# Second pass over a hand-written order: which column runs before the second U columns, pieces in sequence, later value transposes, first weights split on VectorE

## The chip, the cores and the metric

The kernel runs on one core of a Trainium2 chip. The metric is device time in microseconds (us), the median of several runs. One further execution is taken by the hardware profiler; its own time is given beside the runs. Engines are named as in the profile: PE is TensorE's matmul queue and PEld its weight loads, DVE is VectorE, ACT is ScalarE, POOL is GpSimd, SP is SyncE, which here only issues DMAs.

## The reference

One step of a hybrid decoder layer on a prompt of 1024 tokens and on 8 sampled tokens. What matters here is the first stage: the input is normalised, projected with one weight matrix, and a part of the columns (called u) feeds a recurrence over time, RWKV-7.

```
h = rms_norm(x, ln_g) @ w_in                     # 1024 tokens x 3480 columns
q_raw, kv_raw, g_raw, z_nsa, u, z_rw, q_mem, z_mem = split_in(h)
u = u + (previous row of u - u) * mu             # token shift, 896 columns
r, k, v, wl, al = split(u)
decay = exp(-exp(-softplus(-(w0 + tanh(wl) @ w2)) - 0.5))
a = sigmoid(a0 + al @ a2)
kk = normalised per head(k * k_k);  k = k * (1 + (a - 1) * k_a)
for each token t:
    s = s * decay_t + (s @ -kk_t) (kk_t * a_t)^T + v_t k_t^T
    y_t = s @ r_t
shift_prompt = the last row of u
```

The q and k columns are normalised per head (and most of them rotated by position), the z columns go through SiLU. The attention over the results, a step for the samples and an output projection follow; the change does not touch them.

## The kernel before

Matmuls run in a split form: each operand is divided into a high and a low part of a 32-bit format, and a product is three matmuls, high x high, high x low and low x high.

**Weights.** `wblock` brings 128 columns of `w_in`: a DMA of 512 KB on SP's queue into `wraw` (two buffers), the high part `whi` by ACT (L236), the low part `wlo` = raw - high by POOL for six of the eight row blocks and by DVE for two (L238, `LOS = 6`). `whi` and `wlo` have two buffers each, so weights for two columns can be held.

**Projection.** `project(H, ...)` computes such a column for one half of the tokens, H = 0 or 1. Half 0 has 512 prompt tokens and the 8 samples, 520 together, in two PSUM pieces of 256 and 264; half 1 has one piece of 512. It loops over eight row blocks k, and for each k over the three products, and inside these over the pieces. After each k it yields one `STEP` (0.7 us as the kernel reckons). Three PSUM buffers (`pr`) serve it. A half of a column is eight steps.

**The opening.** x of half 0 is loaded, its squares are summed by ACT (`norm_x`), DVE works out the reciprocal roots (L114 to L125) and scales x (L177); PE transposes it, ACT and DVE write the high and low part of h (`make_hT`, L200 and L201). Two weight blocks are brought ahead of the first column (`self.ready`). Here the order of instructions on each engine is left to the tile scheduler, which goes by program order and readiness.

**U columns.** `u_half(H)` projects the seven u columns of a half and evicts them with the token shift (`do_u`: ACT L273, DVE L278 to L283). It is run for half 0 in the opening (line L248 in the profile). Once it is done, the order of PE's instructions is fixed to program order (`InOrder`; its matmuls all have line L83).

**Four quarters.** Each quarter Q of 256 tokens takes `rwkv_prep` and then `rwkv_state`. The prep makes the operands (`p_lora`, `p_vt`, `p_s8`, written `p_s` in the profile, `p_s8t`, `p_rs`, `p_am` are its products on PE, in this order), the state computes a triangular inverse by many small products (`p_iy`, `p_it`) and then the recurrence (`p_x` to `p_z`, `p_yy`). Both are chains over PE, ACT and DVE, so they yield, and `drive` puts steps of other work into PE's order in between: a yield of n lets n x `SLACK` = 1.3 n us of steps in. That other work, the fill, is `columns`: 16 of the remaining columns of `w_in`, each for half 0 and then half 1 with the same weights. The evicted column is turned to token rows and, for q and k columns, normalised on DVE some steps later (`rest`, at the third step of the next half).

**The second U columns.** After the prep of quarter 1, `u_half(1)` is put ahead of the fill, and what the state of quarter 1 hasn't used up runs right behind it. Before that, the fill runs on `while self.open`; `open` is set when a half begins and cleared at the end of each half. Behind the last of these columns `after_u` turns the last row of u around (`p_ul`) and stores it.

Of the kernel before, what the change touches and what calls it, by code (L numbers as in the profile page):

```python
# [32 lines left out]
STEP = 0.7  # L33
SLACK = 1.3
REST = 2
LOS = 6
# [66 lines left out]
class Step:  # L103
# [123 lines left out]
    def wblock(self, c0, n):  # L227

# [4 lines left out]
        self.last_w = nc.sync.dma_start(raw[:, :, :n], src)  # L233
        hi = self.wp.tile([128, 8, 128], F32R, name="whi")
        lo = self.wp.tile([128, 8, 128], F32R, name="wlo")
        nc.scalar.activation(hi[:, :, :n], raw[:, :, :n], AF.Copy)  # L236
        for e, z in ((nc.gpsimd, slice(0, LOS)), (nc.vector, slice(LOS, 8))):
            e.tensor_tensor(lo[:, z, :n], raw[:, z, :n], hi[:, z, :n].bitcast(F32), op=OP.subtract)  # L238
        return hi, lo

    def project(self, H, hi, lo, m, out):
# [3 lines left out]
        for k in range(8):  # L245
            for i, (w, h) in enumerate(((hi, self.hi[H]), (hi, self.lo[H]), (lo, self.hi[H]))):
                for ps, (a, b) in zip(pss, pieces):
                    self.last_mm = self.pe.matmul(ps[:m, :b - a], w[:, k, :m], h[k][:, a:b],  # L248
                                                  start=(k == 0 and i == 0), stop=(k == 7 and i == 2))
            yield STEP  # L250
# [141 lines left out]
    def phase1(self):  # L392
# [8 lines left out]
        with ExitStack() as ctx:  # L401
# [19 lines left out]
            with ExitStack() as xctx:  # L421
# [3 lines left out]
                self.ready = [self.wblock(1816 + j * 128, 128) for j in range(2)]  # L425
                xs1 = self.load_x(1)
                self.norm_x(xs0)
                self.make_hTs()
                for _ in self.make_hT(0):
                    pass  # L430
# [19 lines left out]
            for Q in range(4):  # L450
# [8 lines left out]
                else:  # L459
                    if Q == 3:  # L460
                        uctx.close()
# [37 lines left out]
    def u_half(self, H):  # L499
        self.U = self.up.tile([128, 2, 7, 256], F32, name="U")  # L500
        for j in range(7):
            hi, lo = self.ready.pop(0) if self.ready else self.wblock(1816 + j * 128, 128)
            out = []
            yield from self.project(H, hi, lo, 128, out)
            self.do_u(H, out, j)
        self.after_u(H)

    def columns(self, tiles):

        rest = None  # L510
        for c0, do, j in tiles:
            m = 24 if j is None else 128
            hi, lo = self.wblock(c0, m)
            for H in range(2):
# [8 lines left out]
                self.open = False  # L523
# [4 lines left out]
    def after_u(self, H):  # L528
        nc, O = self.nc, self.O
        if H == 1:  # L530
            ps = self.ptr.tile([128, 512], F32, name="p_ul", tag="tr")
            ul = self.small.tile([128, 7], F32, name="ul7", bufs=1)
            nc.vector.tensor_copy(ul[:], self.ulast[:, :, 0])
            self.pe.transpose(ps[:7, :128], ul[:], self.ident[:])
            o = self.small.tile([8, 128], F32, name="ulo", bufs=1)
            nc.vector.tensor_copy(o[:7], ps[:7, :128])
            dst = O["shift_prompt"]
            nc.sync.dma_start(bass.AP(tensor=dst.tensor, offset=dst.offset, ap=[[128, 7], [1, 128]]), o[:7])
# [42 lines left out]
    def rwkv_prep(self, q):  # L581
# [50 lines left out]
        yield 2.5  # L632
        UV = self.UV = self.rr.tile([128, 4, 4, 64], F32, name="UV")
        pvt = self.pw.tile([128, 2, 4, 64], F32, name="p_vt", tag="w")
        for t in range(2):
            for c in range(2):
# [1465 lines left out]
```

## Time and profile before

| | |
|---|---|
| median of 3 runs | 1178.97 us (1177.57 to 1183.5) |
| the profiled execution | 1185.08 us |
| its span, first to last instruction | 1183.3 us |
| mean granted TensorE clock | 0.973 |
| DMA moved | 102.26 MB, 86 GB/s in the mean |

The span leaves out 1.8 us around the program. How to read the views: the page gives busy time per engine as a share of the span. A row of the waits view says which product on which engine and line waited for whom, the total, how often and the longest. In the timeline a row is start, duration, engine, line, operation, what is written from what is read, and in brackets the idle time before it with what ended it. The windows view gives busy time per engine and the granted clock for a stretch. Matmuls overlap in the pipeline, so the distance of two starts tells their pace, and a busy PE is not PE at its peak. "issue" is a wait for nothing that the profile shows.

### The profile page before, as it was taken

To read this page: it belongs to the slowest core of one execution; us is meant where nothing else is said; L and a number is where in the kernel's file an instruction comes from. 1 tells how busy PE (TensorE), PEld (TensorE's weight loads), DVE (VectorE), ACT (ScalarE), POOL (GpSimd) and SP (SyncE) were. 2 spreads that over 40 slices of the span, in tenths; PEclk is the share of its full clock that TensorE was granted. 3 is DMA by queue.
4 is the path that set the end of the run, shared out by engine and by line. 5 is a ranking of instruction groups with operands and counts; after the bars stand their busy time and mean duration, and the time that the engine had idled before them with its cause. 6 is when DMAs were issued, how large, how long until landed. Compare 5 with 4: busy or idle time off the path is not lost.

```text
span 1183.3 us, 27621 instructions
## 1 busy us (share of the span) xinstructions
PE 1083.9 (92%) x11419; PEld 862.9 (73%) x11419; DVE 728.7 (62%) x2073; ACT 472.4 (40%) x1039; POOL 216.6 (18%) x221
## 2 busy tenths in 40 slices
PE   5998998998799998999998998999999798799998
PEld 4887887766677876777886766777767576677776
DVE  7557377635371594453446699675667886565572
ACT  6342323221322242222425645556566465524420
POOL 3311011112110120021012212022122631101000
PEclk9999999998899999899999999999999899999999
DMA  7322112211221134127136112342200025735321
GB/s 240 88 55 76 36 42 85 56 35 32 61 74 47 28 111 101 39 77 177 46 112 175 50 42 73 121 121 65 79 16 9 29 91 153 243 99 205 128 86 56
DMA packets 124035, 102.26 MB, mean 86 GB/s; under 512 B 33455, under 2 KB 109646, under 8 KB 121734
## 3 DMA queue, kind: packets, MB, share of 16 engines
q1 hardware_dynamic: 119846, 82.50, 24.0%
q0 software_dynamic: 2304, 16.78, 4.1%
q8 instruction: 90, 1.47, 0.5%
q10 hardware_dynamic: 1760, 1.21, 0.3%
q14 instruction: 35, 0.29, 0.1%
HBM read 81.88 MB, written 22.78 MB: 88 GB/s over the span
## 4 chain that ended last, share of the span: by engine, by line
PE 49%; DVE 16%; DMA 5%; ACT 2%; issue 2%; POOL 0%; DVEq 0%; SPq 0%; ACTq 0%; POOLq 0%
PE p_pr L83 7%; PE p_pT L1203 5%; PE p_o L1285 5%; PE p_out L1962 4%; PE p_pr L248 4%; PE p_s L1230 2%; DMA wor<-in_w_out_dram 2%; PE p_s L1231 2%; DMA xg<-in_cache_nsa_dram,idx 2%; PE p_hid L929 1%; DVE nm L1246 1%; PE p_it L83 1%; DVE p L1263 1%; PE p_q L1142 1%; PE p_o L1289 1%
## 5 line engine op out<-in xcount | busy, mean ns | idle before, releaser
L83 PE MATMUL p_pr<-h,whi 128*128 128x256 f32 (+3 forms) x880 | 221.1, 357 | 4.4 <-ACT whi L236 4.1
L83 PEld LDWEIGHTS p_pr<-h,whi 128*128 128x128 f32 (+1 forms) x880 | 136.7, 192 | 25.4 <-ACT whi L236 6.0
L238 POOL TENSOR_TENSOR wlo<-wraw,whi 128x768 fp32r<-128x768 f32 (+1 forms) x35 | 69.7, 1993 | 389.5 <-ACT whi L236 376.9
L83 PE MATMUL p_pr<-h,wlo 128*128 128x512 f32 (+5 forms) x440 | 129.7, 343 | 8.2 <-POOL wlo L238 8.2
L248 PE MATMUL p_pr<-h,whi 128*128 128x256 f32 (+2 forms) x464 | 95.1, 312 | 3.7 <-DVE ulast L283 1.9
L1285 PE MATMUL p_o<-pt,vs 128*64 128x128 f32 x1056 | 92.5, 286 | 3.8 <-ACT pt L1207 1.5
L1265 POOL TENSOR_TENSOR p<-p,fac 128x640 f32<-128x640 f32 (+4 forms) x64 | 62.2, 993 | 170.6 <-DVE fac L1259 82.8
L83 PEld LDWEIGHTS p_pr<-h,wlo 128*128 128x128 f32 (+1 forms) x440 | 76.3, 192 | 20.4 <-POOL wlo L238 10.8
L1230 PE MATMUL p_s<-kh,qs 128*128 128x512 f32 (+3 forms) x192 | 77.8, 406 | 9.6 <-ACT p L1247 8.9
L1203 PE MATMUL p_pT<-ident,p 128*128 128x128 f32 x528 | 83.6, 288 | 2.0 <-DVE pt L1209 1.1
L1285 PEld LDWEIGHTS p_o<-pt,vs 128*64 128x64 f32 x1056 | 58.6, 137 | 27.3 <-issue 14.5
L248 PEld LDWEIGHTS p_pr<-h,whi 128*128 128x128 f32 x464 | 71.9, 193 | 8.7 <-issue 4.4
L1203 PEld LDWEIGHTS p_pT<-ident,p 128*128 128x128 f32 x528 | 58.6, 144 | 18.7 <-issue 14.5
L236 ACT ACTIVATE whi<-wraw 128x1024 fp32r<-128x1024 f32 (+1 forms) x35 | 36.3, 1038 | 85.9 <-PE p_pr L83 55.5
L1246 DVE TENSOR_REDUCE nm<-p_s 128x1 f32<-128x640 f32 (+3 forms) x64 | 58.6, 918 | 15.6 <-PE p_s L1233 15.3
L1247 ACT ACTIVATE p<-p_s,nm 128x640 f32<-128x640 f32 (+3 forms) x64 | 55.9, 873 | 30.3 <-DVE nm L1246 28.1
L1231 PE MATMUL p_s<-kl,qs 128*128 128x512 f32 (+3 forms) x192 | 65.5, 346 | 0.0
L1207 ACT ACTIVATE pt<-p_pT 128x512 f32<-128x512 f32 (+1 forms) x72 | 42.6, 591 | 54.0 <-PE p_pT L1203 53.6
L238 DVE TENSOR_TENSOR wlo<-wraw,whi 128x256 fp32r<-128x256 f32 (+1 forms) x35 | 18.7, 533 | 72.5 <-ACT whi L236 72.3
L248 PE MATMUL p_pr<-h,wlo 128*128 128x256 f32 (+2 forms) x232 | 61.7, 308 | 1.1 <-POOL wlo L238 1.1
L1209 DVE COPY pt<-p_pT 128x512 f32<-128x512 f32 (+1 forms) x72 | 47.7, 663 | 20.5 <-PE p_pT L1203 20.1
L1962 PE MATMUL p_out<-wol,chi 128*128 128x512 f32 x128 | 51.6, 403 | 0.2 <-DVE wol L1952 0.2
(532 smaller groups left out, 2317.1 us busy)
## 6 DMA issues: line engine op xcount, KB each, us to landing
wraw<-in_w_in_dram SPq DMA_DIRECT2D x34, 512.0 KB
x<-in_x_prompt_dram SPq DMA_DIRECT2D x8, 512.0 KB
z_d<-zt SPq DMA_DIRECT2D x16, 256.0 KB
cat<-z_d SPq DMA_DIRECT2D x8, 512.0 KB
wor<-in_w_out_dram SPq DMA_DIRECT2D x16, 256.0 KB
xres<-in_x_prompt_dram SPq DMA_DIRECT2D x16, 256.0 KB
out_dram<-xres SPq DMA_DIRECT2D x16, 256.0 KB
out_dram<-in_cache_win_dram SPq DMA_DIRECT2D x8, 511.0 KB
```

The costliest lines, as they stand in the source:

```text
L83: self.last = getattr(self.engine, op)(*a, **k)
L238: e.tensor_tensor(lo[:, z, :n], raw[:, z, :n], hi[:, z, :n].bitcast(F32), op=OP.subtract)
L248: self.last_mm = self.pe.matmul(ps[:m, :b - a], w[:, k, :m], h[k][:, a:b], start=(k == 0 and i == 0), stop=(k == 7 and i == 2))
L1203: nc.tensor.transpose(ps[:, j, :], src(j), self.ident[:])
L1209: nc.vector.tensor_copy(pt[:, :n], ps[:, :n])
L1230: PE.matmul(ps, q, self.kh[u][:, 2 * b + g, o:o + w], start=True, stop=False)
L1231: PE.matmul(ps, q, self.kl[u][:, 2 * b + g, o:o + w], start=False, stop=not masks)
L1246: V.tensor_reduce(nm[:, h, b:b + 1], ps[:, c0:n1], axis=AX.X, op=OP.max, negate=True)
L1247: A.activation(Ps[h, b][:, :n1 - c0], ps[:, c0:n1], AF.Exp, bias=nm[:, h, b:b + 1], accum_out=sm[:, h, b:b + 1])
L1265: nc.gpsimd.tensor_tensor(x, x, bc(f[:, h, b:b + 1], x.shape), op=OP.mult)
L1285: PE.matmul(po[h * 64:h * 64 + 64], self.vs[k // 4][:, k % 4, b, g], pt[:, 2 * m + h], start=(n == 0 and m == 0), stop=False)
L1962: nc.tensor.matmul(po[:rows], c[:, k, :rows], w[:], start=(k == 0 and j == 0), stop=(k == 7 and j == 2))
```

## The change

Six edits, all in the first stage:

- `wblock` is divided into the load and the split. The two first blocks are loaded where they were, but split after the normalisation of x and the samples' h, and with `los = 0`: the low part is DVE's alone.
- `project` runs the pieces of half 0 one behind the other, eight k each, and not interleaved, but for the very first column. It still yields eight times.
- `open` is cleared only after half 1, so the column that is under way is finished for both halves ahead of the second U columns.
- `after_u` becomes `last_u` and moves from behind the last second U column to between prep and state of quarter 2.
- In `rwkv_prep` the four transposes of the values (`p_vt`) and the copy `vt` move from ahead of `p_s8` to behind the reciprocal root that follows `p_s8t`. The yields change from 1.0, 2.5, 2.5, 1.2, 4.0, 5.5 to 1.0, 4.0, 2.0, 5.0, 5.5.
- One more yield of 1.0 stands behind the four `p_am`.

```diff
     def wblock(self, c0, n):
+        return self.w_split(self.w_load(c0, n), n)
+
+    def w_load(self, c0, n):
...
         self.last_w = nc.sync.dma_start(raw[:, :, :n], src)
+        return raw
+
+    def w_split(self, raw, n, los=LOS):
...
-        for e, z in ((nc.gpsimd, slice(0, LOS)), (nc.vector, slice(LOS, 8))):
+        for e, z in ((nc.gpsimd, slice(0, los)), (nc.vector, slice(los, 8))):
+            if z.start == z.stop:
+                continue
             e.tensor_tensor(lo[:, z, :n], raw[:, z, :n], hi[:, z, :n].bitcast(F32), op=OP.subtract)
         return hi, lo
 
-    def project(self, H, hi, lo, m, out):
+    def project(self, H, hi, lo, m, out, first=False):
...
-        for k in range(8):
+        parts = [(ps, a, b, k) for ps, (a, b) in zip(pss, pieces) for k in range(8)]
+        if first:
+            parts.sort(key=lambda x: x[3])
+        for n, (ps, a, b, k) in enumerate(parts):
             for i, (w, h) in enumerate(((hi, self.hi[H]), (hi, self.lo[H]), (lo, self.hi[H]))):
-                for ps, (a, b) in zip(pss, pieces):
-                    self.last_mm = self.pe.matmul(ps[:m, :b - a], w[:, k, :m], h[k][:, a:b],
-                                                  start=(k == 0 and i == 0), stop=(k == 7 and i == 2))
-            yield STEP
+                self.last_mm = self.pe.matmul(ps[:m, :b - a], w[:, k, :m], h[k][:, a:b],
+                                              start=(k == 0 and i == 0), stop=(k == 7 and i == 2))
+            if H or n % 2:
+                yield STEP
...
                 xs0 = self.load_x(0)
-                self.ready = [self.wblock(1816 + j * 128, 128) for j in range(2)]
+                raws = [self.w_load(1816 + j * 128, 128) for j in range(2)]
                 xs1 = self.load_x(1)
                 self.norm_x(xs0)
                 self.make_hTs()
+                self.ready = [self.w_split(raw, 128, 0) for raw in raws]
                 for _ in self.make_hT(0):
...
                 else:
+                    if Q == 2:
+                        self.last_u()
                     if Q == 3:
                         uctx.close()
                     self.drive(self.rwkv_state(Q), fill)
...
-            yield from self.project(H, hi, lo, 128, out)
+            yield from self.project(H, hi, lo, 128, out, (H, j) == (0, 0))
             self.do_u(H, out, j)
-        self.after_u(H)
...
                 rest = do(H, out, j)
-                self.open = False
+                self.open = H == 0
                 yield STEP
...
-    def after_u(self, H):
+    def last_u(self):
...
-        yield 2.5
+        yield 4.0
         UV = self.UV = self.rr.tile([128, 4, 4, 64], F32, name="UV")
-        pvt = self.pw.tile([128, 2, 4, 64], F32, name="p_vt", tag="w")
-        for t in range(2):
-            for c in range(2):
-                PE.transpose(pvt[:, t, 2 * c:2 * c + 2, :].rearrange("p a b -> p (a b)"),
-                             vs[:, c, t * 128:(t + 1) * 128], self.ident[:])
-        vt = self.rp.tile([128, 2, 4, 64], F32, name="vt", tag="rk")
-        A.activation(vt[:], pvt[:], AF.Copy)
-        yield 2.5
         ps8 = self.pw.tile([128, 512], F32, name="p_s8", tag="w")
...
-        yield 1.2
+        yield 2.0
...
         V.tensor_scalar(rsb[:], bc(rs[:, :, None], [128, 8, 64]), 1e12, None, op0=OP.min)
+        pvt = self.pw.tile([128, 2, 4, 64], F32, name="p_vt", tag="w")
+        for t in range(2):
+            for c in range(2):
+                PE.transpose(pvt[:, t, 2 * c:2 * c + 2, :].rearrange("p a b -> p (a b)"),
+                             vs[:, c, t * 128:(t + 1) * 128], self.ident[:])
+        vt = self.rp.tile([128, 2, 4, 64], F32, name="vt", tag="rk")
+        A.activation(vt[:], pvt[:], AF.Copy)
         A.activation(UV[64:, 0::2], vt[64:], AF.Copy)
         A.activation(UV[:64, 1::2], vt[:64], AF.Copy)
-        yield 4.0
+        yield 5.0
...
                 yield 0.5
+        yield 1.0
```

More of the change, by code (lines that the diff above doesn't have):

```diff
@@ L233, in wblock @@
         self.last_w = nc.sync.dma_start(raw[:, :, :n], src)
+        return raw
+    def w_split(self, raw, n, los=LOS):
+        nc = self.nc
         hi = self.wp.tile([128, 8, 128], F32R, name="whi")
@@ L526, in columns @@
             rest()
-    def after_u(self, H):
+    def last_u(self):
         nc, O = self.nc, self.O
[L530 to L538, printed above, removed]
+        ps = self.ptr.tile([128, 512], F32, name="p_ul", tag="tr")
+        ul = self.small.tile([128, 7], F32, name="ul7", bufs=1)
+        nc.vector.tensor_copy(ul[:], self.ulast[:, :, 0])
+        self.pe.transpose(ps[:7, :128], ul[:], self.ident[:])
+        o = self.small.tile([8, 128], F32, name="ulo", bufs=1)
+        nc.vector.tensor_copy(o[:7], ps[:7, :128])
+        dst = O["shift_prompt"]
+        nc.sync.dma_start(bass.AP(tensor=dst.tensor, offset=dst.offset, ap=[[128, 7], [1, 128]]), o[:7])
     def rwkv_pools(self, P):
```

## The prediction

> **What bounds the kernel now.** I read the page first: busy share by engine, then the slices. One row carries it.
>
> ```profile
> PE 1083.9 (92%) x11419; PEld 862.9 (73%) x11419; DVE 728.7 (62%) x2073; ACT 472.4 (40%) x1039; POOL 216.6 (18%) x221
> ```
>
> PE, the matmul queue, is busy 1083.9 of 1183.3 us, and none of its work is removed. So the change is worth the time in which PE stands still, plus what PE loses to a lower clock behind such stretches. All edits act on the first stage, where the PE order is written by hand. I therefore asked for PE's waits from 20 to 460 us; a row is the waiting product, who released it, total us, times, longest.
>
> ```profile
> PE p_pr L83 <- POOL wlo L238: 8.2, 6, 2.4
> PE p_iy L83 <- DVE AM L702: 5.2, 7, 2.2
> PE p_pr L83 <- ACT whi L236: 4.1, 5, 1.0
> PE p_ul L83 <- DVE ul L533: 3.8, 1, 3.8
> PE p_rs L83 <- DVE rsb L657: 3.5, 2, 3.3
> PE p_vt L83 <- ACT vs L610: 3.1, 2, 2.4
> PE p_s8t L83 <- DVE s L646: 2.6, 2, 1.7
> PE p_pr L248 <- DVE ulast L283: 1.9, 4, 0.7
> ```
>
> The largest item is weights that come too late: 8.2 + 4.1 = 12.3 us. All of it lies in the second U columns: one column of the fill was left half done, keeps one of the two weight buffers, and so each U column can only be split after the one before it has ended. The windows view shows what that does (us, busy of PE, PEld, DVE, ACT, POOL, granted clock, DMA share, GB/s).
>
> ```profile
> 282.00:290.00 8.00, 6.57 (x17) 5.18 (x18) 4.00 (x9) 0.63 (x1) 3.58 (x4) 0.57 0.33 98
> 291.50:300.00 8.50, 6.13 (x24) 4.36 (x24) 2.42 (x5) 1.65 (x3) 2.05 (x1) 1.00 0.23 64
> ```
>
> A column has 24 matmuls. Between 291.5 and 300.0 it takes 8.5 us, of which PE works 6.13, and behind the longest wait the granted clock is 0.57.
>
> **The second U columns (column finished ahead).** The timeline of PE gives where the dense run of U steps begins, the price of a step, and what follows the last column.
>
> ```profile
> 275.56 0.74 PE L83 MATMUL p_pr<-h,whi 128*128 128x512 f32 x2
> ...
> 296.26 0.63 PE L83 MATMUL p_pr<-h,whi 128*128 128x512 f32 x2
> ...
> 296.97 0.63 PE L83 MATMUL p_pr<-h,whi 128*128 128x512 f32 x2
> ...
> 313.65 0.38 PE L83 MATMUL p_ul<-ident,ul 128*7 128x128 f32 x1 [3.77 <-DVE ul L533]
> 313.68 1.20 PE L83 MATMUL p_pr<-h,whi 128*128 128x512 f32 x2
> ```
>
> A step (three matmuls of 512) is 0.71 us at full clock. The run from 275.6 ends 3.77 before 313.65, at 309.9: 34.3 us for the last 29 U steps, which at 0.71 are 20.6. So **13.7 saved** is the most here. The least is the waits alone; the same view of waits, for the recurrence of quarter 1 before that run (217 to 276 us), parts them.
>
> ```profile
> PE p_pr L83 <- POOL wlo L238: 3.0, 3, 1.4
> PE p_pr L83 <- ACT whi L236: 1.2, 2, 1.0
> ```
>
> 4.2 of the 12.3 lie in the recurrence, 8.1 in the run: bounds 8.1 and 13.7. I take the upper end, for the rest of it is the slow clock that stands behind the waits. In the recurrence the waits may cover round trips of its own chain that will show instead: of 4.2 I take **3.1** (bounds 0 and 4.2).
>
> Can the columns really follow without a wait? The timeline behind the last U column shows one split and the eviction of a column:
>
> ```profile
> 309.74 1.06 ACT L236 ACTIVATE whi<-wraw 128x1024 fp32r<-128x1024 f32 x1 [8.33 <-PE p_pr L83]
> 310.70 0.67 ACT L273 ACTIVATE U<-p_pr,dv 128x512 f32<-128x512 f32 x1
> 310.83 0.42 DVE L238 TENSOR_TENSOR wlo<-wraw,whi 128x256 fp32r<-128x256 f32 x1 [7.39 <-ACT whi L236]
> 310.87 2.04 POOL L238 TENSOR_TENSOR wlo<-wraw,whi 128x768 fp32r<-128x768 f32 x1 [7.91 <-ACT whi L236]
> 311.41 0.48 DVE L280 SCALAR_TENSOR_TENSOR U<-p_pr,vec,U 128x255 f32<-128x255 f32 x1 [0.15 <-ACT U L273]
> 311.81 1.12 DVE L281 SCALAR_TENSOR_TENSOR U<-ulast,vec,U 128x1 f32<-128x1 f32 x1
> ```
>
> Once a buffer is free, the split is done from 309.74 to 312.91, 3.2 us, beside a column of 8 x 0.71 = 5.7. The next block's load starts when its raw buffer is freed; in the windows view:
>
> ```profile
> 283.80:288.30 4.50, 4.50 (x12) 3.44 (x12) 2.20 (x7) 0.63 (x1) 2.20 (x3) 0.50 0.51 146
> ```
>
> At 146 GB/s the 512 KB move within those 4.5 us, and they are needed 8 us later. The slack is 2.5 us; what else POOL does in a column must fit in there. The forced steps of the finished column are the same work done earlier.
>
> At the turn into quarter 2, `p_ul` no longer stands in front: its 3.77 us go, its matmul is issued before state 2, when the input is long there, and its small store on SP moves with it. Late next is the first `p_lora`, which needs tanh of the last U column: 0.67 + 0.48 + 1.12 (0.16 for one column where POOL is quiet, as the opening's rows show) and tanh, an estimated 0.4 from the 0.67 for twice the columns, are 1.7 to 2.7 us, and two steps (1.4) cover them. A new wait of 0.3 to 1.3; I take 0.6. The two steps behind `p_ul` run at half pace (1.20 for 0.63), 1.3 more to save. **3.8 - 0.6 + 1.3 = 4.5** (bounds 1, if the new wait lets the clock drop again, and 5).
>
> [...]
>
> **The opening (first weights split on VectorE).** The timeline there:
>
> ```profile
> 12.35 3.81 POOL L238 TENSOR_TENSOR wlo<-wraw,whi 128x768 fp32r<-128x768 f32 x2 [1.01 <-ACT whi L236]
> 12.64 1.77 DVE L125 SCALAR_TENSOR_TENSOR rq_r<-rq_t,rq_g 128x1 f32<-128x1 f32 x1
> ...
> 16.20 0.16 DVE L125 SCALAR_TENSOR_TENSOR rq_r<-rq_t,rq_r 128x1 f32<-128x1 f32 x1
> ...
> 17.72 2.64 PE L197 MATMUL p_h<-ident,x 128*128 128x128 f32 x10 [4.14 <-DVE x L177]
> ```
>
> The nearest row for a whole split on DVE, from the groups (busy us, mean ns), has the same size and two operands:
>
> ```profile
> L1309 DVE TENSOR_TENSOR pmem<-pmem,sm_m 128x1024 f32<-128x1024 f32 x8 | 9.7, 1218 | 0.1
> ```
>
> While POOL's two subtractions run, 3.81 us, a DVE operation on one column takes 1.77 us, and its like takes 0.16 once they are over, and PE waits 4.14 us for the scaled x behind it. One such stall for each subtraction gives 3.2 saved without them. DVE gets two full subtractions at 1.22 for two parts of 0.42: 1.6 added. DVE is the engine everything there waits for, so I take **1.5**. Bounds: 4, PE's whole wait, if both splits fall into gaps; -1.6 if x comes no earlier.
>
> **Pieces one behind the other.** It applies to token half 0, two pieces in two PSUM banks. Could 24 matmuls in a row into one bank cost something? A stretch of the interleaved form, PE on these products alone:
>
> ```profile
> 36.47:42.30 5.83, 5.83 (x49) 1.00 0.43 127
> ```
>
> 5.83 us for 48 matmuls of 256 columns (one of the next falls in) are 0.73 for six; three of 512 into one bank took 0.71. No loss, and every matmul has its own weight load either way (11419 of each on the page). The gain is the first piece's earlier eviction, against 1.9 us of waits for it in the first U columns. Those also depend on where ACT and DVE queue the eviction, so **1.0** (bounds 0 and 1.9).
>
> **Preparations (values' transposes later).** A yield of n lets the fill run 1.3n us in steps of 0.7. Before `p_s8t` there were 7.2 units, now 7.0: 14 steps each time. Before `p_rs` 11.2 become 12.0, two steps more. Four transposes move behind `p_s8t`, where `vs` is long ready, so the 3.1 us for `p_vt` go. But what is late next?
>
> ```profile
> 177.40:191.20 13.80, 9.69 (x48) 7.25 (x47) 13.69 (x45) 5.88 (x12) 3.62 (x4) 0.88 0.10 31
> ```
>
> DVE works 13.69 of 13.80 us between the wait for `p_vt` and the one for `p_s8t`. PE only arrives at `p_s8t` earlier and waits there, so in quarter 1 I count nothing. In quarter 0 the two later steps cover 1.4 of `p_rs`' longest, 3.3. **1.5 saved.** The upper bound is all waits of the three, 3.1 + 2.6 + 3.5 = 9.2. Below nothing it reaches as far as one more head normalisation ahead of these products:
>
> ```profile
> 485.43 0.69 DVE L317 TENSOR_REDUCE nr_ss<-nr_sq 128x8 f32<-128x512 f32 x1 [3.78 <-ACT nr_sq L315]
> ...
> 493.82 0.41 DVE L339 TENSOR_TENSOR nr_o<-nr_o,nr_sq 128x256 f32<-128x256 f32 x1
> ```
>
> It holds DVE's queue for 8.8 us from first to last, with little between; two steps cover 1.4 of it: -7.
>
> The new yield of 1.0 behind `p_am` puts two steps (1.4 us) between the masks and the recurrence, in each quarter. Also, by counting columns, the fill between `p_rs` and `p_am` in quarters 2 and 3 becomes a z column, with no normalisation, where it was a q column. So of 5.2 us of `p_iy` waiting for `AM` I take **4.5** (bounds 0, and 8.8 with the clock behind them, in the proportion of 13.7 to 8.1).
>
> **The end of the stage.** 28 steps of fill were left behind quarter 3, about 12 will be. They cover the loads of the next stage, which no row prices. Between 0 and the longest wait that the first stage shows, 4.1, I take the middle: **-2**.
>
> **Sum:** 13.7 + 3.1 + 4.5 + 1.5 + 1.0 + 1.5 + 4.5 - 2 = 27.8 us. The profiled execution took 1185.08 (span 1183.3, 1.8 around it): 1157. Its time is 6.1 above the median of the runs, 1178.97; on that scale **1151 us**.
>
> **The rivals.**
> - *The preparations take it back.* DVE is full there; normalisations land ahead of `p_s8t` and `p_rs`. The preparations' 1.5 becomes -7 and the masks' 4.5 becomes 0: 27.8 - 13 = 15, so 1164. For it: the 13.69. Against it: only quarter 1 is that full.
> - *The column ahead does not free the weights in time.* If POOL's output tiles (`y_c`) or the load stretch the split beyond the column, 13.7 + 3.1 is lost: 11 saved, 1168. Against it: 3.2 beside 5.7.
> [...]
> - *Slower: DVE becomes the bound of every preparation.* One further normalisation of 8.8 us ahead of `p_rs` in all four adds 35 us to PE's waits: 1178.97 - 27.8 + 35 = 1186. It decides from 7 us per quarter on. Against it: the number of normalisations is the same, only their places move.
>
> **How the numbers follow.** Forecast 0.60, preparations 0.20, weights 0.10, clock 0.06, slower 0.04. The range reaches from 1139 (every term at its upper bound but the preparations', 39 saved) to 1169, which takes in the first three rivals. A measurement of this kernel tells about 0.5%, 5.9 us, from no change. Faster by more: the forecast and the first three rivals, 0.96, less 0.05 where the first two of these meet (27.8 - 13 - 17 = -2); within: those 0.05; slower: 0.04.
>
> **What would show it.** Right: no wait of `p_pr` for `whi` or `wlo` in the second U columns, 29 steps in about 21 us at clock 1.00, no `p_ul` wait, and no DVE operation of 1.7 us near 13 us. Wrong: waits for `p_s8t` or `p_rs` longer than the 9 us that went, or U columns still over 7 us each.

## The result and the profile after

| | before | changed |
|---|---|---|
| median | 1178.37 us (4 runs, 1177.57 to 1183.5) | 1138.72 us (4 runs, 1133.44 to 1143.41) |
| ratio | | 0.9653, 95% interval 0.9603 to 0.9704 |
| profiled execution, span | 1185.08, 1183.3 | 1133.44, 1131.7 |

The change saves 39.7 us at the medians, where 27.8 were forecast. 1138.7 lies 12.3 us under the forecast of 1151 and 0.3 under the low end of the range. The busy row of the page shows that no work went:

```profile
PE 1062.0 (94%) x11419; PEld 848.6 (75%) x11419; DVE 728.0 (64%) x2073; ACT 475.0 (42%) x1039; POOL 219.0 (19%) x219
```

The counts of PE and DVE are the same as before; PE's busy time fell by 21.9 us for the same matmuls. That is the first sign of the clock: a matmul at half clock counts as busy, and longer (in the profile before, two of 512 columns took 1.20 us at 313.68, at clock 0.50, and 0.63 at 296.26, at 1.00). (The profiled execution before is slower than all four of its runs and the changed one is the fastest of its four, so sizes are taken from all runs further down.) The waits of PE in the first stage, 20 to 460 us (product, releaser, total, times, longest):

```profile
PE p_rs L83 <- DVE rsb L663: 8.2, 4, 2.9
PE p_lora L83 <- ACT U L603: 2.2, 1, 2.2
PE p_it L83 <- issue: 2.1, 3, 0.9
PE p_it L83 <- DVE iY L735: 1.9, 3, 0.8
PE p_pr L83 <- issue: 1.3, 2, 0.8
PE p_pr L260 <- DVE ulast L296: 1.0, 1, 1.0
PE p_g L83 <- DVE UV L801: 0.7, 1, 0.7
```

No wait for `whi`, `wlo`, `p_ul`, `p_vt`, `p_s8t` or `AM` is left. `p_rs` waits longer than before (8.2 for 3.5), and `p_lora` is new. The windows view of the dense run and of the turn behind it (us, busy of PE, PEld, DVE, ACT, POOL, granted clock, DMA share, GB/s):

```profile
263.50:286.60 23.10, 23.05 (x112) 18.82 (x111) 16.30 (x50) 7.85 (x11) 10.90 (x10) 1.00 0.28 80
286.40:289.80 3.40, 1.21 (x7) 0.95 (x6) 2.26 (x6) 0.97 (x3) 1.76 (x1) 1.00 0.14 29
289.80:293.20 3.40, 3.40 (x14) 3.03 (x13) 2.21 (x5) 1.68 (x4) 0.00 (x0) 0.50 0.42 126
293.20:296.60 3.40, 3.40 (x30) 3.40 (x29) 3.00 (x6) 2.94 (x6) 0.00 (x0) 1.00 0.42 128
```

PE is full for the whole dense run, at clock 1.00. Then it stands still for 2.19 us at the new `p_lora` wait, and the next 3.4 us run at 0.50: 14 matmuls, where the same stretch takes 28 at clock 1.00 in the first experiment (there from 293.2 to 296.6 us).

Each run also has a span and a mean granted clock, so the gain can be split without a trace. Span x (1 - clock) is what half clock costs if PE is the bound. From all runs that have a clock on record (means, us; the first experiment has the changed kernel's order and is counted with it; two slow runs of the kernel before are left out):

| | runs | span | lost to the clock | rest |
|---|---|---|---|---|
| before | 44 | 1180.4 | 31.9 | 1148.5 |
| changed | 10 | 1139.6 | 14.4 | 1125.2 |
| saved | | 40.8 | 17.5 | 23.3 |

The forecast holds the same two parts: 6.9 for the clock (13.7 - 8.1 in the dense run, 1.3 at the turn) and 20.9 for waits. The waits are right within 2.4 us as a sum, in part by luck, as the single terms will show. The clock is short by 10.6.

The split has an uncertainty of its own. The rest of the kernel before is the same in each of four batches of runs, 1148.2 to 1149.0; its loss to the clock is 30.4 to 31.4 in three of them and 34.6 in the fourth. In the batch of the first experiment alone, the change saves 15.6 in the clock and 21.7 in the rest.

### The profile page after: what moved, and what is told of

Read it like the earlier page. It is cut to its first block, busy times and chain, and to the rows that moved or that the text cites. A ratio compares the mean times of both kernels' runs of the same rounds, so it can differ in the third digit from the quotient of the medians.

```text
span 1131.7 us, 27604 instructions
## 1 busy us (share of the span) xinstructions
PE 1062.0 (94%) x11419; PEld 848.6 (75%) x11419; DVE 728.0 (64%) x2073; ACT 475.0 (42%) x1039; POOL 219.0 (19%) x219
## 4 chain that ended last, share of the span: by engine, by line
PE 60%; DVE 15%; DMA 4%; ACT 3%; issue 2%; POOL 0%; SPq 0%; DVEq 0%; ACTq 0%; POOLq 0%
PE p_pr L83 12%; PE p_out L1976 6%; PE p_o L1299 5%; PE p_pT L1217 5%; PE p_pr L260 4%; PE p_s L1244 2%; PE p_s L1245 2%; PE p_it L83 2%; DMA xg<-in_cache_nsa_dram,idx 2%; PE p_hid L943 1%; DVE nm L1260 1%; DMA wor<-in_w_out_dram 1%; PE p_am L83 1%; PE p_yy L83 1%; PE p_z L83 1%
## 5 line engine op out<-in xcount | busy, mean ns | idle before, releaser
L83 PE MATMUL p_pr<-h,whi 128*128 128x512 f32 (+5 forms) x880 | 225.4, 347 | 1.3 <-issue 1.3
L83 PEld LDWEIGHTS p_pr<-h,whi 128*128 128x128 f32 (+1 forms) x880 | 140.0, 185 | 19.6 <-issue 3.2
L83 PE MATMUL p_pr<-h,wlo 128*128 128x512 f32 (+5 forms) x440 | 145.5, 331 | 0.0
L260 PE MATMUL p_pr<-h,whi 128*128 128x264 f32 (+2 forms) x464 | 98.9, 309 | 1.0 <-DVE ulast L296 1.0
L83 PEld LDWEIGHTS p_pr<-h,wlo 128*128 128x128 f32 (+1 forms) x440 | 81.3, 185 | 10.5 <-issue 1.1
L260 PEld LDWEIGHTS p_pr<-h,whi 128*128 128x128 f32 x464 | 74.7, 190 | 5.2 <-ACT U L286 1.2
L260 PE MATMUL p_pr<-h,wlo 128*128 128x256 f32 (+2 forms) x232 | 70.7, 305 | 1.2 <-POOL wlo L248 1.2
L1261 ACT ACTIVATE p<-p_s,nm 128x640 f32<-128x640 f32 (+3 forms) x64 | 55.9, 874 | 30.4 <-DVE nm L1260 28.2
L1976 PE MATMUL p_out<-woh,clo 128*128 128x512 f32 x128 | 51.8, 405 | 0.0
L1976 PE MATMUL p_out<-woh,chi 128*128 128x512 f32 x128 | 51.6, 404 | 0.0
```

The source lines that it names most:

```text
L83: self.last = getattr(self.engine, op)(*a, **k)
L1261: A.activation(Ps[h, b][:, :n1 - c0], ps[:, c0:n1], AF.Exp, bias=nm[:, h, b:b + 1], accum_out=sm[:, h, b:b + 1])
L1976: nc.tensor.matmul(po[:rows], c[:, k, :rows], w[:], start=(k == 0 and j == 0), stop=(k == 7 and j == 2))
```

## The experiments

Two explanations of the missing 12 us were tested: A, the waits that went took more half clock with them than was counted; B, one of the six edits is worth more than its term. The table above already speaks for A, but only for the sum. Each edit was therefore undone alone. In the following, "lost to the clock" and "rest" are means over the runs as above, against 14.4 and 1125.2 for the changed kernel. The medians of one kernel in different batches differ by some us, so ratios are compared; for the loss to the clock, the kernel before of the same batch is the better yardstick.

### The column ahead, undone

```diff
-                self.open = H == 0
+                self.open = False
```

> The changed kernel, but a column of the first token half is no longer finished ahead of the second half's columns; all else stays. Theory A (every wait of PE that went took a stretch of half clock with it, 3.4 us long and worth 1.7, and only part of these was counted): the second-half columns wait for whi and wlo again, 8 to 9 us, about four half-clock stretches come back, and the time is 16 to 19 us above the changed kernel's 1138.7, about 1156, ratio to the kernel before 0.981. Theory B (the dense second-half columns bring more than 13.7 + 3.1, and the other edits what was predicted): 24 us or more above, 1163 or later, ratio 0.987 or more. Theory C (the other edits leave the weights in time anyway): under 6 us above.

Measured 1142.6 us, 0.9673 (0.9629 to 0.9717). The traces of the two kernels hold the same instructions in the same order on every engine. With the new yields the fill stands in the second half of a column when quarter 1 ends, so either form of `open` stops at the same step. This edit does nothing in this kernel by itself; theory C of the expectation holds. As a second set of runs of the same order it has another use. Windows of both traces, the changed kernel first:

```profile
154.20:161.00 6.80, 6.80 (x71) 6.24 (x72) 3.11 (x11) 0.00 (x0) 1.35 (x1) 1.00 0.43 123
```

```profile
154.20:161.00 6.80, 6.80 (x41) 6.12 (x41) 1.89 (x7) 0.00 (x0) 1.35 (x1) 0.50 0.44 123
...
289.80:293.20 3.40, 1.21 (x7) 0.96 (x6) 2.25 (x6) 0.96 (x3) 1.76 (x1) 1.00 0.13 19
```

The same code runs 71 matmuls in 6.8 us at clock 1.00 in one execution and 41 at 0.50 in the other; and the wait at the turn, which brought half clock above, brought none here (the stage has no other stretch at 0.50). So the wait alone doesn't decide. The last section comes back to it.

### The column ahead, alone

The kernel before with this one edit.

```diff
-                self.open = False
+                self.open = H == 0
```

> The kernel before with one edit: the column under way is finished for both halves ahead of the second-half columns. The prediction priced this at 13.7 + 3.1 = 16.8 us, waits and the half clock in the dense run together. If that term holds: ratio to the kernel before 0.984 to 0.988, no wait of p_pr for whi or wlo, the dense run at 0.71 us a step. If the later preparations also lose half-clock stretches by it, 20 us or more, 0.983 or less. Rival: quarter 1 loses the cover of these steps and its own waits grow by 5 us or more, ratio 0.992.

Measured 1168.88 us, 0.9885 (0.9842 to 0.9928): 13.6 us, with 16.8 inside the interval (8.5 to 18.6); the ratio itself lies just above the expected 0.984 to 0.988. The waits for `whi` and `wlo` are gone from its list, and the dense run is as full as in the changed kernel; windows and waits of this kernel:

```profile
270.00:296.00 26.00, 26.00 (x152) 21.73 (x151) 18.43 (x58) 7.05 (x11) 10.42 (x9) 1.00 0.19 51
```

```profile
PE p_rs L83 <- DVE rsb L657: 8.6, 3, 3.3
PE p_vt L83 <- ACT vs L610: 4.7, 2, 2.5
...
PE p_ul L83 <- DVE ul L533: 3.8, 1, 3.8
...
PE p_iy L83 <- DVE AM L702: 0.4, 2, 0.2
```

From the last `p_yy` ahead of the dense run to the first `p_lora` behind it the profiles have 41.0 us before, 26.6 here and 24.3 in the changed kernel (the latter two with two steps more), so in this stretch the mechanism is as predicted. Lost to the clock: 28.7, which is 5.9 less than the kernel before in the same batch (3.2 less than all its runs); the rest fell by 7.6. Outside the stretch the edit moves the fill: the waits for `AM` fall from 5.2 to 0.4 us without a new yield (the prediction's other reason for that term, a column without normalisation ahead of the masks, would give this; it wasn't followed), while those for `p_rs` and `p_vt` grow (8.6 for 3.5, 4.7 for 3.1) and still bring half clock (stretches at 326.2 and 425.1 us; with that behind `p_ul` at 302.3, 13.7 us in all). What is needed is that the column is finished when the second U columns begin; either this edit or the new yields give that.

### The preparation, undone

Order and yields of `rwkv_prep` as before; the rest as changed.

```diff
-        yield 4.0
+        yield 2.5
...
+        pvt = self.pw.tile([128, 2, 4, 64], F32, name="p_vt", tag="w")
...
+        yield 2.5
...
-        yield 2.0
+        yield 1.2
...
-        yield 5.0
+        yield 4.0
...
-        yield 1.0
```

> The changed kernel with the preparation of the kernel before: its yields, the values' transposes ahead of p_s8t, no last yield. The prediction gave the preparations 1.5 and the masks 4.5, so 6 us come back if its sizes hold: 1145, ratio 0.971. Theory A (half-clock stretches uncounted): the waits for vt, AM and s8t come back, 9 to 12 us, with four or five half-clock stretches at 1.7: 12 to 17 us above the changed kernel, 1151 to 1156, ratio 0.977 to 0.981. Theory B (the dense second-half columns alone are worth the surplus): 6 us or less.

Measured 1153.41 us, 0.9754 (0.9707 to 0.9802): 9.6 us above the first experiment's ratio, 11.9 above that of the changed kernel. The waits of its trace:

```profile
PE p_rs L83 <- DVE rsb L671: 9.2, 3, 3.6
...
PE p_vt L83 <- ACT vs L624: 4.8, 2, 2.5
PE p_s8t L83 <- DVE s L660: 3.2, 1, 3.2
```

The rest rises by 9.8, the clock's share by 2.3. By its time it lies in theory A's interval; by its ratio, which is what can be compared, it lies between the 0.971 of the prediction's sizes and theory A's 0.977 to 0.981. It isn't A's mechanism either: most of the loss is standing still. The wait for `AM`, which I expected back, is 0.4 us in all here.

### The last yield, undone

```diff
-        yield 1.0
```

> The changed kernel without the last yield of a preparation, so no steps of fill stand between p_am and the recurrence. The prediction gave the masks' waits 4.5 us. If its size holds: p_iy waits for AM again, 4 to 5 us in all, and the time is 4 to 5 us above the changed kernel's 1139 to 1143. If each of these waits also takes half-clock windows: 3 to 4 such windows more in the stage than the changed kernel's two, and 8 to 12 us above. Rival: the steps only move, and under 2 us change.

Measured 1149.54 us, 0.9689 (0.9653 to 0.9725), 1.9 to 4.2 us above the changed kernel, near the 4.5 of the forecast. The mechanism of the forecast isn't there: the list of waits names no `AM`, so the size was met by luck. The rest rises by 2.6. The clock's share is 5.1 above that of the changed kernel, but this is the batch in which the kernel before, too, loses most to the clock (34.6), so what of it is the edit's is not shown. Its profile has seven half-clock windows in the first 500 us where the changed kernel's has two, yet the time isn't the 8 to 12 us above that were expected with so many. Of its waits, two of the largest; the second is one of `p_iy`, but for nothing that the profile shows:

```profile
PE p_rs L83 <- DVE rsb L663: 9.1, 4, 4.0
...
PE p_iy L83 <- issue: 3.6, 2, 2.2
```

### The first weights, undone

```diff
-                raws = [self.w_load(1816 + j * 128, 128) for j in range(2)]
+                self.ready = [self.wblock(1816 + j * 128, 128) for j in range(2)]
...
-                self.ready = [self.w_split(raw, 128, 0) for raw in raws]
```

> The changed kernel with the first two weights split where they load, six parts in eight on POOL. Predicted worth 1.5 us; the two profiles show PE's first product only 0.7 us earlier. Theory A and the profiles: 0.7 to 1.5 us above the changed kernel, within what can be told; a DVE operation on one column takes 1.7 us again near 13 us, and PE waits 4.1 us for x. Rival: the first columns also wait for wlo behind POOL, and 3 us or more come back.

Measured 1145.45 us, 0.9697 (0.9652 to 0.9742), 2.8 to 5.2 above, which the intervals don't tell from none. The trace does: the first `p_pr` starts at 20.80 us here, at 19.60 in the changed kernel and at 20.29 before, and over all profiles at 18.90 to 19.66 with the new split (12 profiles) and at 20.29 to 20.99 with the old one (4). DVE and PE in this kernel, then PE in the changed one:

```profile
13.16 1.77 DVE L125 SCALAR_TENSOR_TENSOR rq_r<-rq_t,rq_g 128x1 f32<-128x1 f32 x1
...
14.96 1.72 DVE L121 SCALAR_TENSOR_TENSOR rq_t<-rq_r,rq_a 128x1 f32<-128x1 f32 x1
```

```profile
18.24 2.64 PE L197 MATMUL p_h<-ident,x 128*128 128x128 f32 x10 [4.66 <-DVE x L177]
```

```profile
17.04 2.63 PE L197 MATMUL p_h<-ident,x 128*128 128x128 f32 x10 [3.48 <-DVE x L177]
```

The means of the two groups lie 1.4 us apart, 1.5 were predicted. With POOL's subtraction back, an operation on one column takes 1.77 us again near 13 us; its like in the same kernel takes 0.16 at 16.72.

### The pieces, undone

```diff
-        parts = [(ps, a, b, k) for ps, (a, b) in zip(pss, pieces) for k in range(8)]
-        if first:
-            parts.sort(key=lambda x: x[3])
-        for n, (ps, a, b, k) in enumerate(parts):
+        for k in range(8):
...
+                for ps, (a, b) in zip(pss, pieces):
```

> The changed kernel with the two pieces of a column interleaved weight by weight, as before. Predicted worth 1.0 us; the profiles show that the first six columns end 5.3 us earlier than the first product's 0.7 explains. If the pieces' order makes that: 5 to 6 us above the changed kernel, 1144, ratio 0.971, columns at 6.8 in place of 6.2 us. If it is the split on POOL that slowed these columns: under 1.5 us, and columns stay at 6.2.

Measured 1153.57 us, 0.9765 (0.9713 to 0.9817): 10.9 to 13.2 above. This is the surprise among the edits; 1.0 was predicted. The rest rises by 6.5, the clock's share by 6.6. Windows in the opening, this kernel first, then the changed one:

```profile
48.00:54.00 6.00, 5.60 (x48) 5.43 (x47) 2.99 (x10) 3.00 (x5) 2.08 (x1) 1.00 0.25 64
```

```profile
48.00:54.00 6.00, 6.00 (x53) 6.00 (x52) 2.82 (x9) 2.48 (x4) 2.09 (x1) 1.00 0.27 76
```

48 matmuls against 53 in 6 us, both at full clock: 0.4 us of standing still in each column, behind the eviction of the column before. A column starts every 6.8 us, in sequence every 6.2, as expected. The timeline of ACT shows why, first interleaved, then in sequence:

```profile
49.66 0.83 ACT L283 ACTIVATE U<-p_pr,dv 128x256 f32<-128x256 f32 x2
```

```profile
49.81 0.46 ACT L286 ACTIVATE U<-p_pr,dv 128x256 f32<-128x256 f32 x1
51.61 0.48 ACT L286 ACTIVATE U<-p_pr,dv 128x256 f32<-128x256 f32 x1 [1.34 <-PE p_pr L260]
```

Interleaved, both pieces end within 0.5 us and are evicted together (one row, x2). A column takes two of three PSUM buffers, so the next one has one until an eviction is done. In sequence the row at 49.81 is the second piece of one column, and that at 51.61 already the first piece of the next: it ended at 51.58, and PE computes the second piece until 54.5. So the two evictions of a column lie 4.4 us apart (51.61 and 56.01). The waits that go (this kernel):

```profile
PE p_pr L258 <- DVE ulast L293: 3.3, 6, 1.4
...
PE p_h L197 <- DVE h L201: 1.3, 1, 1.3
```

From the first `p_pr` to the first `p_lora`, the interleaved kernels take 54.8 (before), 53.9 (the column ahead alone) and 54.1 us (this one); the changed kernel takes 49.5, the first experiment 48.8. 4.6 to 5.2 us are the edit's there. The other half of the measured difference lies in the clock (11.5 to 33.7 us lost in the six runs) and wasn't followed to its places; the interval doesn't exclude that it is smaller.

### Waits put in: short and long

To test the clock itself, round trips from PE to DVE and back are added to the dense run, where the changed kernel has no wait. Short: a copy and two operations on DVE, after every fourth step. Long: a copy and nine, in the middle of a column.

```diff
+    def gap(self, k):
+        V = self.nc.vector
+        ps = self.ptr.tile([128, 512], F32, name="p_gap", tag="tr")
+        self.pe.transpose(ps[:8, :128], self.ident[:, :8], self.ident[:])
+        g = self.small.tile([8, 128], F32, name="gap", bufs=1)
+        V.tensor_copy(g[:, :128], ps[:8, :128])
+        for _ in range(k):
+            V.tensor_scalar(g[:], g[:], 1.0, None, op0=OP.mult)
+        self.pe.transpose(ps[:, 128:136], g[:, :128], self.ident[:8, :8])
...
-                    for _ in second:
-                        pass
+                    for n, _ in enumerate(second):
+                        if n % 4 == 2:
+                            self.gap(2)
```

The long form has `n % 8 == 4` and `gap(9)`.

> The changed kernel with extra round trips PE to DVE and back put into the dense second-half columns, which otherwise run without a wait: one after every fourth step, seven or eight in all, each an estimated 0.9 us of standing still. The clock theory (a window of 3.41 us with over 2 us of idle PE is always followed by one at half clock, one with under 1.25 almost never): no half-clock window in the dense run, and its 24.1 us grow by the gaps alone, to about 31. Rival (each wait, short or long, lowers the clock): three or more half-clock windows there, and 36 us or more.

> The same, with a longer chain on DVE: one round trip in the middle of every column, three or four in all, each an estimated 3 us. The clock theory: a window at half clock behind nearly each of them, so the dense run's 24.1 us grow by the gaps and 1.7 us for each window at half clock, to 36 to 43 for four gaps (9 to 12 of gaps and three or four windows). Rival (the clock does not follow the gaps): no half-clock window beyond chance, and 33 to 36 us.

The round trips were longer than estimated. PE's timeline, short form, then long:

```profile
272.00 0.22 PE L83 MATMUL p_gap<-ident,gap 8*128 8x8 f32 x1 [0.94 <-DVE gap L551]
...
280.18 0.22 PE L83 MATMUL p_gap<-ident,gap 8*128 8x8 f32 x1 [4.84 <-DVE gap L551]
...
285.93 0.22 PE L83 MATMUL p_gap<-ident,gap 8*128 8x8 f32 x1 [0.87 <-DVE gap L551]
...
292.01 0.22 PE L83 MATMUL p_gap<-ident,gap 8*128 8x8 f32 x1 [2.74 <-DVE gap L551]
...
302.28 0.22 PE L83 MATMUL p_gap<-ident,gap 8*128 8x8 f32 x1 [2.74 <-DVE gap L551]
```

```profile
275.60 0.27 PE L83 MATMUL p_gap<-ident,gap 8*128 8x8 f32 x1 [6.66 <-DVE gap L551]
...
289.13 0.27 PE L83 MATMUL p_gap<-ident,gap 8*128 8x8 f32 x1 [5.11 <-DVE gap L551]
```

Short: seven gaps, 13.9 us in all, and one stretch of half clock, behind the gap of 4.84. The six others, 0.9 to 2.7 us, brought none; the dense run with its turn, 24.1 us in the changed kernel, takes 43.3. Long: four gaps, 22.0 us, and a stretch of 6.8 us of half clock that begins 1.4 to 1.7 us before the end of each gap; 54.1 us, where 36 to 43 were expected. Windows, short form then long:

```profile
280.50:283.90 3.40, 3.40 (x9) 2.66 (x10) 0.00 (x0) 0.00 (x0) 0.00 (x0) 0.50 0.51 152
283.90:309.00 25.10, 17.01 (x77) 12.41 (x76) 8.19 (x25) 4.12 (x5) 4.08 (x2) 1.00 0.16 42
```

```profile
273.90:280.70 6.80, 5.10 (x13) 4.02 (x14) 2.14 (x13) 0.63 (x1) 2.19 (x3) 0.50 0.35 99
```

Both estimates failed on the gaps' length, not on the clock: the rival of the short form, half clock behind each wait, would have put it behind all seven, and that of the long form, a clock that doesn't follow the gaps, not behind four of four.

### The kernel before, once more

> The kernel before, unchanged, profiled once more. Theory A (half-clock windows stand on a free-running grid, so which waits cost one differs from execution to execution, but their number stays high while the waits are there): 8 to 12 half-clock windows in the first 500 us, not all at the same places as in the first profile (12), and the waits the same to some tenths. Rival (the first profile was an outlier and the half clock isn't the change's gain): 5 windows or fewer.

One execution, 1189.13 us, of a span of 1187.4 at a mean clock of 0.966. The longest waits are those of the first profile to 0.1 us, and the first 500 us hold 11 half-clock windows against 12. But the places of the 11 are the same too, 0.7 us later each, against what I expected: the grids of windows of the two executions happen to lie only 0.7 us apart. So the 12 were no outlier.

### p_rs later

In the changed kernel `p_rs` has the longest waits. Three kernels try to take them away, one fills the turn, one does both.

```diff
-        yield 5.0
+        yield 7.0
...
-        yield 5.5
+        yield 4.0
```

> The changed kernel with p_rs later: the yields 5.0 and 5.5 around it become 7.0 and 4.0, three or four steps of fill more ahead of p_rs. Its four waits, 8.2 us in all and the longest of the stage, go or fall under 2 us, and with them the one or two half-clock windows behind them: 5 to 10 us faster than the changed kernel, ratio 0.958 to 0.962. Rival (p_am then waits for the operands that DVE makes behind p_rs): the waits move to p_am, and within 3 us of the changed kernel.

Measured 1145.4 us, 0.9683 (0.9648 to 0.9718): no gain, though the waits for `p_rs` fell from 8.2 to 1.2 us and the rest from 1125.2 to 1121.0. The clock takes it back: 22.3 lost, for 14.4. PE's timeline and the windows of quarter 2:

```profile
320.69 1.13 PE L83 MATMUL p_am<-ar,bk 64*128 64x128 f32 x8 [1.39 <-DVE ar L684]
...
322.76 2.07 PE L83 MATMUL p_am<-ar,bk 64*128 64x128 f32 x8
```

```profile
322.40:325.80 3.40, 3.40 (x16) 2.94 (x15) 1.99 (x6) 0.63 (x1) 0.15 (x1) 0.51 0.58 132
325.80:329.20 3.40, 3.40 (x15) 2.95 (x15) 1.17 (x3) 0.38 (x1) 0.00 (x0) 0.50 0.28 99
329.20:332.60 3.40, 3.40 (x15) 2.94 (x15) 0.54 (x3) 0.00 (x0) 0.00 (x0) 0.50 0.00 0
332.60:336.00 3.40, 3.40 (x17) 3.31 (x17) 2.08 (x6) 0.35 (x1) 0.00 (x0) 0.50 0.00 0
```

`p_am` now waits 1.39 us, and from the next window on four in a row are at half clock, without a further wait: eight `p_am` take 2.07 us, not 1.13. They use 64 rows, where `p_pr` has 128. Quarter 3 has another stretch of 13.65 us at the same place. So the rival holds: 3.6 us of waits moved to `p_am`, and the time is 1.2 to 3.5 us above the changed kernel's.

> The changed kernel with 7.0 in place of 5.0 ahead of p_rs, and 5.5 kept behind it, so p_am comes later too. If a wait right ahead of p_am is what holds the clock at half through the p_am products (13.65 us twice with 7.0 and 4.0), it goes: no wait of p_am over 0.5 us, no half-clock stretch longer than 6.8 us in the preparations, the mean loss to the clock back at 14 us or under from 22, and the time 4 to 8 us below the changed kernel, ratio 0.959 to 0.963. Rival (the steps taken here are missing behind the last recurrences, where the fill runs out): waits of the recurrence of quarter 3 grow by as much, ratio 0.965 or more.

Here it is 7.0 and 5.5, so `p_am` comes later as well. Measured 1143.22 us, 0.9672 (0.9638 to 0.9705). The first half of the expectation holds in the main: `p_am` doesn't wait, no stretch in the preparations is over 6.8 us, and the clock's share falls to 16.4, where 14 or under was expected. The other half doesn't: the rest is 1124.3, and the waits stand in the recurrences, such as:

```profile
PE p_it L83 <- DVE iY L781: 3.3, 2, 1.7
...
PE p_it L83 <- DVE rq_r L125: 1.9, 1, 1.9
```

> The same with 6.0 and 5.5: two steps more ahead of p_rs than the changed kernel, half of what the other adds. The four waits of 2.2, 0.6, 2.5 and 2.9 us shrink to about 0.8, 0, 1.1 and 1.5, which a 3.41-us window stands without half clock: 3 to 6 us below the changed kernel, ratio 0.961 to 0.963. Rival: normalisations of the fill move ahead of the operands that p_rs needs, its waits stay over 2 us, ratio 0.965 or more.

Measured 1145.09 us, 0.9694 (0.9670 to 0.9718). `p_rs` still waits 4.2 us, longest 2.3; the rival holds. That a window stands a wait of 1.5 us is also not sure: in the 16 profiles 45 of 134 windows with 1.25 to 2.0 us of idle PE had half clock behind them.

### The turn filled, and both

```diff
+                if Q == 2:
+                    for _ in range(4):
+                        next(fill)
                 self.drive(self.rwkv_prep(Q % 2), fill)
```

> The changed kernel with four more steps of fill between the last second-half column and the preparation of quarter 2. The wait of p_lora for tanh, 2.19 us, goes, and the half-clock window that stood behind it in most profiles: 2 to 4 us faster than the changed kernel. Rival: the normalisations of the fill column move behind p_s8t or p_rs in quarter 2, whose waits grow by as much; no change.

> p_rs later and the turn filled, both on the changed kernel: 8 to 13 us faster than it if both hold and are independent, ratio 0.955 to 0.960, with no wait over 2 us left between 20 and 460 us and at most two half-clock windows there. Rival (what is gained at p_rs is lost at p_am): ratio 0.963 or more.

Alone: 1146.03 us, 0.9705 (0.9677 to 0.9732). `p_lora` no longer waits, but the fill behind it stands four steps further on, and `p_rs` and `p_s8t` of quarter 3 wait 3.7 and 2.1 us. With `p_rs` later (7.0 and 4.0): 1142.39 us, 0.9666 (0.9638 to 0.9694); waits of 3.2 (`p_rs`) and 2.1 us (`p_s8t`) are left, where none over 2 was expected. The five lie between 0.9666 and 0.9705, beside 0.9653 and 0.9673 for the changed order, so none is shown to be faster.

## Why the prediction was right or wrong

- **What bounds the kernel** was right: standing still in the first stage and the clock behind it. The step that failed is the size of the clock's term. I priced half clock at two places only, 5.6 in the dense run and 1.3 at the turn, and gave the waits of the opening, the recurrence, the preparations and the masks their bare length, though the upper bound of the masks' term (8.8) had a price for it. The runs have 17.5 in place of 6.9 (15.6 in the batch of the first experiment). The profile of before had shown it: of its 12 half-clock windows in the first 500 us the dense run and the turn hold four. Of the other eight, one stands at the wait for `p_rs` (98.1 us), one behind that for `p_vt` (180.0) and three behind waits for `AM` (357.5, 453.1, 473.5). The changed kernel's profile has two in all, behind `p_lora` (289.8) and `p_rs` (313.7). The low end of the range is a little off as well: the upper bounds sum to 39.1, which is 1139.9 and not 1139.
- **The waits' sum**, 20.9 against 23.3 measured, is closer than its terms, so in part it is luck. With the edits undone one by one, the rest moves by 6.5 for the pieces (1.0 forecast), by 9.8 for preparations and masks (6.0), and by 7.6 for the column ahead alone (8.1 + 3.1).
- **The dense run**, 13.7 + 3.1: held within the measurement, alone 13.6 (8.5 to 18.6), which includes what the edit does to the waits of the preparations and of `AM`. That it was the column ahead that gives it was half right: the new yields give it too.
- **The turn**, 4.5: too high. The wait of `p_ul` (3.77) went, but `p_lora` waits 2.19 where I took 0.6, so the waits give 1.6 us where 3.2 were priced, and half clock stood behind it in six of the ten profiles that have this wait. It is the lower bound of that step, "1, if the new wait lets the clock drop again". The chain, as the timeline of the changed kernel shows it:

```profile
284.98 1.06 ACT L244 ACTIVATE whi<-wraw 128x1024 fp32r<-128x1024 f32 x1 [3.96 <-PE p_pr L83]
285.95 0.67 ACT L286 ACTIVATE U<-p_pr,dv 128x512 f32<-128x512 f32 x1
288.27 0.75 ACT L603 ACTIVATE U<-U 64x256 f32<-64x256 f32 x2 [1.66 <-DVE U L294]
```

```profile
286.08 0.42 DVE L248 TENSOR_TENSOR wlo<-wraw,whi 128x256 fp32r<-128x256 f32 x1 [3.00 <-ACT whi L244]
286.65 0.48 DVE L293 SCALAR_TENSOR_TENSOR U<-p_pr,vec,U 128x255 f32<-128x255 f32 x1 [0.15 <-ACT U L286]
287.05 1.13 DVE L294 SCALAR_TENSOR_TENSOR U<-ulast,vec,U 128x1 f32<-128x1 f32 x1
```

  My sum took the operation on one column at 1.12 with POOL and 0.16 without; the next block's split is on POOL just there (2.04 us from 286.12), and it took 1.13. And it began with the eviction, but ACT first splits the next block's weights (1.06): the column's last product ends near 285.1, the eviction starts at 285.95. The rows of the prediction had that order, L236 at 309.74 and L273 at 310.70. So the chain is 3.6 us, not 2.7 at most, beside the same 1.4 of cover.
- **The opening**, 1.5: 1.4 in the traces.
- **The pieces**, 1.0: the second step that failed. 4.6 to 5.2 us in the opening alone. I counted only the 1.9 us of waits in the U columns' row. Waits that carry other names at the same place, 1.4 (`rq_r`) and 1.3 (`p_h`), belong to it: the interleaved kernel has 4.6 us of waits there under two names, the changed one 1.0. A bound of 1.9 was too low; the rest of the difference stands in no wait that the view names.
- **The preparations and masks**, 1.5 + 4.5: together 9.6 to 11.9 measured. The last yield alone is right in size (1.9 to 4.2) and not in mechanism: the waits for `AM` are down to 0.4 us or none in all three kernels that lack it and have another of the edits. What the yield is worth comes from elsewhere, and from where stays open.
- **The end of the stage**, -2: no loss seen. From the last `p_yy` of quarter 3 on, the profile of before takes 671.9 us and the changed one 649.3, 22.6 less. 16 steps less of fill (11.4) and 10.2 us less of half clock (5.1) leave a gain of 6.1 us; the second profiles of both orders, 677.7 and 655.1 with 22.5 us less of half clock, leave none. So a loss of 2 isn't excluded.
- **The rivals.** "The preparations take it back", "the weights still late" and "slower" didn't occur; only the waits for `p_rs` grew, by 4.7 us. The chance of 0.06 for the clock, the third rival that the range takes in, was for a slow clock that the waits don't make. The put-in waits and the split of the gain speak against it (half clock at all four long gaps, 17.5 of 40.8 us saved), though a few stretches stand behind no wait (14 behind windows with under 1.25 us of idle PE in the 16 profiles).

So both explanations hold in part: A, the clock, for 9 to 11 us, and B, in the pieces, for about 4, against which the turn and the end of the stage count with a few us in either direction. How the 15.6 to 17.5 us of the clock divide among the edits stays open beyond the figures above, since they don't simply add.

## What to carry over

Price a wait of TensorE by its length and by the half clock that it may bring; here the second came to some three quarters of the first (17.5 us saved beside 23.3). Read span x (1 - mean clock) of every run beside the waits of one profile. With two pieces of a product and three PSUM buffers, as here, run the pieces one behind the other, so that the first is evicted while the second is computed: 4.6 to 5.2 us in the opening here.

## What the hardware showed

**Half clock came in whole windows of 3.413 us.** The starts of the half-clock stretches in a profile lie whole numbers of 3.413 us apart: in that of before 74.2, 98.1, 180.0 and 234.6 are 7, 24 and 16 such windows from each other, and stretches last 3.41, 6.83 or 10.24 us. Over the 16 profiles, by the idle PE time of a window at full clock and what the next one got:

| idle PE in a window of 3.41 us | windows | next at half clock |
|---|---|---|
| under 1.25 us | 4877 | 14 |
| 1.25 to 2.0 us | 134 | 45 |
| 2.0 us and more | 73 | 73 |

From 2.0 us of idle PE in one window on, the next one was at half clock in all 73 cases. The phase differs between executions: the grid begins 0.1 to 3.4 us behind the start of the span (2.5 in the profile before, 3.1 in the changed one). Where a wait lay on the grid went with what followed it. At the turn all of `p_lora`'s 2.19 us lay in one window in the changed kernel's profile and half clock followed; in the first experiment they fell into 0.81 and 1.39, and the two gaps of 2.74 into 1.45 and 1.29, and 1.42 and 1.32, and none followed. That fits with how equal programs differ: from 10 to 21 us lost to the clock in ten runs of the changed order.

**Half clock without a wait stood at small products.** In the kernel with `p_rs` later, once it was low, it stayed low for 13.65 us without a wait, twice, while `p_am` on 64 rows ran between the steps of fill, and 8 of the 14 cases under 1.25 us lie between 151 and 157 us, in the small products of a recurrence. In the changed kernel the same `p_am` ran at full clock and didn't lower it (323 to 330 us, clock 1.00, eight in 1.16 us). This is seen; that the products are the cause wasn't tested.
